# Adaptive vectors from one row sum of products per 128 outputs, and the short convolution's input projection with seven products of quarters

## The chip, the cores and the metric

The kernel runs on one core of a Trainium2 chip. Time is device time of one launch in microseconds (us). A row of a profile names engines: PE multiplies matrices, DVE (VectorE) and ACT (ScalarE) work element by element, POOL is GpSimd, SP issues most of the DMA transfers. A tile of the text "128x512" has 128 partitions of 512 elements; an instruction handles all partitions at once.

## What is computed

The reference is a backbone of two layers over 512 latent tokens of width 1024, with 256 context tokens ahead of layer 0. Cut to what the change touches:

```python
mod = silu(c) @ ada_w[layer] + ada_b[layer]        # 1024 -> 6144, per layer
shift_m, scale_m, gate_m, shift_f, scale_f, gate_f = split(mod, 6)
h = modulate(rms_norm(x), shift_m, scale_m)        # h * (1 + scale) + shift
# layer 0: attention and a gated recurrence on h @ ev_w_in, then @ ev_w_out
# layer 1: the short convolution
gate_b, gate_c, u = split(h @ od_w_in, 3)          # 1024 -> 3 * 1024
y = (gate_b * dwconv3(gate_c * u)) @ od_w_out
x = x + gate_m * y
h = modulate(rms_norm(x), shift_f, scale_f)
x = x + gate_f * ((gelu(dwconv3(a)) * val) @ ffn_w_down)   # a, val = split(h @ ffn_w_up, 2)
```

So each layer needs a vector `mod` of 6144 numbers, 48 columns of 128, and only the norms, the projections back and the final residual read it. All arithmetic is in fp32 to the outside. Inside, a product of matrices is made of three products: each operand is split into a high part and a low part (the rounding rest), and high times high, high times low and low times high are added up.

## The kernel before, in words

**Stages.** The profile shows them one after another: a prologue with the first 16 columns of layer 0's `mod`, the input norms and the projection of the first six heads' gates (0 to 65 us); the gated recurrence, woven by `Weave` with the remaining input projections (to about 245); attention, woven likewise (to about 380); the projection back `o0` (`project_back`, to 418); layer 0's up projection `ffn_up` (418 to 652); the projection back `d0` (652 to 784); the short convolution (784 to 917); its projection back `o1` (to 962); layer 1's up projection (to 1197); layer 1's down projection with the final norm.

**What sets the order.** Each engine runs its own queue in order. The queues come from the program's order through the tile framework, which also puts in the waits. A tile of a pool with `bufs=n` waits for the reader of the n-th tile before it. Weights come by one plan: `Weights._load` (L57) brings 1 MB at a time into two buffers `wraw`, `conv` (L69) casts a part to its high half `whi` on ACT (L92) and takes the rest `wlo` on DVE (L93), three buffers each, so conversions run a little ahead of the products. All three products are issued by `mm3` (L288 to L290).

**Adaptive vectors (`Ada`, L474 to L527).** All but the prologue's 16 columns are made in 160 units, eight for each of 20 jobs of 512 outputs. A unit loads 256 KB of `ada_w` (128 inputs by 512 outputs, three buffers `ar`), and DVE multiplies it by the 128 inputs (one number per partition) and adds it to `aa` (L502 for the first of eight, L504 for the others). After the eighth, DVE sums blocks of 32 partitions (`ad`, L508); three unit calls later PE sums the four blocks (`pad`, L514, with the constant `sel`), and two calls later DVE adds the bias from PSUM in four small additions (L520). The calls are scattered over the program: `ada_units` in the two weaves, `units(4)` or `units(5)` in each step of a projection back, `units(3)` after each pair of the short convolution, `units(2)` per group in layer 1's up projection.

**Up projection of an FFN.** The first four tiles go through `quad` (L1103). The rest goes in ten groups, `group` (L1151): a product of a 2x2 block matrix by seven products of quarters (Strassen's scheme, in Winograd's form with sums and differences of quarters), plus a plain product for the other half of the inputs. A group makes two pairs of output tiles and takes 84 half-width (256) and 48 full-width (512) matmuls. Its differences of weights are made on DVE by `_block` (L100; L108 to L114 the sums, L125 and L126 the casts), its differences of activations once per layer by `differences` (L1121). Results leave PSUM by copies (L1176) and additions (L1181, L1201).

**The short convolution.** `quad` makes the first two tiles of `gate_c` and of `u`; then ten calls of `pair` (L1095), each two tiles with 48 full-width matmuls: `gate_b` of j = 0, then `gate_c`, `u` and `gate_b` for j = 1 to 3. ACT copies `gate_c` to `cs` (L1287), DVE multiplies it by `u` (L1295), convolves (`conv3`, L1212 to L1214) into `sc`, and multiplies by `gate_b` (L1305), after which the result is split for `o1`.

**End of the prologue.** The products `pq` of the gates' projection (PE, `mm3`), then DVE makes `qh` from `pq` (L461), `gg` (L280), and, from `context` (L319), the modulated context tokens (L313, L314, L324). PE goes on with `pvl` (L577), the first product of the recurrence's stage. At the other end of the program L1323 and L1324 turn a gate vector into a row: a diagonal matrix `dgb` on DVE, multiplied by `ones` on PE into `pgb`, then copied to `gb` (L1325).

## Time and profile before

| | us |
|---|---|
| three runs before | 1333.11, 1334.85, 1336.33 (median 1334.85) |
| the profiled execution | 1333.99 |
| its span on the engines | 1332.2 |
| PE busy | 1304.5 |
| DVE busy | 965.4 |
| ACT busy | 625.2 |

The profiled execution lies 0.86 us below the median of the runs, and 1.8 us of it lie outside the span. In a row of a timeline stand start, duration, engine, line, operation, output<-inputs, the matmul's array, the output's shape and count, and in brackets the idle time before it and what ended that. A matmul's duration is longer than its pitch, the time to the next one's start, as PE overlaps them. A row of groups has the total, then the mean in ns of one, then idle time and what released it. A row of waits has the total, the number of times and the longest. A row of windows has for each engine its busy time and number of instructions, then the mean clock granted to PE (1.00 is full), the DMA engines' busy share and GB/s.

### The profile page before, as it was taken

To read this page: it belongs to the slowest core of one execution; us is meant where nothing else is said; L and a number is where in the kernel's file an instruction comes from. 1 tells how busy PE (TensorE), PEld (TensorE's weight loads), DVE (VectorE), ACT (ScalarE), POOL (GpSimd) and SP (SyncE) were. 2 spreads that over 40 slices of the span, in tenths; PEclk is the share of its full clock that TensorE was granted. 3 is DMA by queue.
4 is the path that set the end of the run, shared out by engine and by line. 5 is a ranking of instruction groups with operands and counts; after the bars stand their busy time and mean duration, and the time that the engine had idled before them with its cause. 6 is when DMAs were issued, how large, how long until landed. Compare 5 with 4: busy or idle time off the path is not lost. (4 is left out here: it accounts for less than half of the span.)

```text
span 1332.2 us, 21229 instructions
## 1 busy us (share of the span) xinstructions
PE 1304.5 (98%) x8456; PEld 1147.6 (86%) x8456; DVE 965.4 (72%) x1688; ACT 625.2 (47%) x1085; POOL 84.3 (6%) x87
## 2 busy tenths in 40 slices
PE   7999999999999999999999999999999999999997
PEld 4798888888779998889877898888999989899997
DVE  4668897887778878788766776667789897782333
ACT  4443445555545656565422253223456565663223
POOL 2204332311000000000000000000000000000000
PEclk9999999999999999999999999999999999999999
DMA  9842113674562122323466734555403423242231
GB/s 293 265 123 84 33 33 82 152 182 134 153 206 96 64 99 92 127 71 119 141 211 198 226 132 143 167 165 174 158 27 117 142 80 127 80 146 69 91 108 64
DMA packets 134995, 172.35 MB, mean 129 GB/s; under 512 B 14320, under 2 KB 103792, under 8 KB 129776
## 3 DMA queue, kind: packets, MB, share of 16 engines
q1 hardware_dynamic: 132896, 166.15, 39.3%
q10 hardware_dynamic: 2000, 4.85, 1.4%
q8 instruction: 66, 1.08, 0.3%
q14 instruction: 33, 0.27, 0.1%
HBM read 165.21 MB, written 2.10 MB: 126 GB/s over the span
## 5 line engine op out<-in xcount | busy, mean ns | idle before, releaser
L92 ACT CAST whi<-wraw 128x1024 fp32r<-128x1024 f32 (+1 forms) x122 | 124.1, 1021 | 280.8 <-PE pd L1340 70.4
L93 DVE TENSOR_TENSOR wlo<-wraw,whi 128x1024 fp32r<-128x1024 f32 (+1 forms) x122 | 145.2, 1192 | 107.7 <-ACT whi L92 107.1
L288 PE MATMUL p<-hf,whi 128*128 128x512 f32 (+1 forms) x640 | 215.4, 338 | 1.4 <-ACT whi L125 1.4
L290 PE MATMUL p<-hf,wlo 128*128 128x512 f32 (+1 forms) x640 | 214.6, 335 | 0.0
L289 PE MATMUL p<-hf,whi 128*128 128x512 f32 (+1 forms) x640 | 214.1, 335 | 0.0
L125 ACT CAST whi<-wraw 128x512 fp32r<-128x512 f32 (+1 forms) x160 | 113.0, 727 | 85.0 <-PE p L289 35.0
L290 PEld LDWEIGHTS p<-hf,wlo 128*128 128x128 f32 x640 | 120.1, 188 | 13.6
L288 PEld LDWEIGHTS p<-hf,whi 128*128 128x128 f32 x640 | 120.1, 188 | 12.3 <-ACT whi L125 1.6
L289 PEld LDWEIGHTS p<-hf,whi 128*128 128x128 f32 x640 | 120.1, 188 | 10.7
L126 DVE TENSOR_TENSOR wlo<-wraw,whi 128x512 fp32r<-128x512 f32 (+1 forms) x160 | 128.1, 817 | 0.9 <-ACT whi L125 0.5
L504 DVE SCALAR_TENSOR_TENSOR aa<-ar,sil,aa 128x512 f32<-128x512 f32 x140 | 104.8, 749 | 24.1 <-DMA ar<-in_ada_w_dram 21.8
L1339 PE MATMUL pd<-whi,g 128*128 128x256 f32 x352 | 98.2, 279 | 0.0
L1341 PE MATMUL pd<-wlo,g 128*128 128x256 f32 x352 | 98.1, 279 | 0.0
L1340 PE MATMUL pd<-whi,g 128*128 128x256 f32 x352 | 97.9, 278 | 0.0
L288 PE MATMUL pbd<-g,whi 128*128 128x512 f32 (+1 forms) x192 | 73.5, 383 | 0.0
L289 PE MATMUL pbd<-g,whi 128*128 128x512 f32 (+1 forms) x192 | 73.3, 382 | 0.0
L290 PE MATMUL pbd<-g,wlo 128*128 128x512 f32 (+1 forms) x192 | 73.1, 381 | 0.0
L288 PE MATMUL p<-T,whi 128*128 128x256 f32 x240 | 69.0, 288 | 0.0
L290 PE MATMUL p<-T,wlo 128*128 128x256 f32 x240 | 67.2, 280 | 0.0
L289 PE MATMUL p<-T,whi 128*128 128x256 f32 x240 | 67.2, 280 | 0.0
L1340 PEld LDWEIGHTS pd<-whi,g 128*128 128x128 f32 x352 | 66.3, 188 | 0.0
L1339 PEld LDWEIGHTS pd<-whi,g 128*128 128x128 f32 x352 | 66.1, 188 | 0.0
(679 smaller groups left out, 3296.3 us busy)
## 6 DMA issues: line engine op xcount, KB each, us to landing
ar<-in_ada_w_dram SPq DMA_DIRECT2D x160, 256.0 KB, 3.1
wraw<-in_upq_dram SPq DMA_DIRECT2D x40, 1024.0 KB, 4.8
wraw<-in_ffn_w_down_dram SPq DMA_DIRECT2D x16, 1024.0 KB, 5.3
wraw<-in_od_w_in_dram SPq DMA_DIRECT2D x12, 1024.0 KB, 5.6
wraw<-in_ev_w_in_dram SPq DMA_DIRECT2D x20, 512.0 KB, 5.2
araw<-in_ada_w_dram SPq DMA_DIRECT2D x16, 512.0 KB, 6.3
wraw<-in_ffn_w_down_dram SPq DMA_DIRECT2D x8, 768.0 KB, 4.7
wraw<-in_ev_w_out_dram SPq DMA_DIRECT2D x4, 1024.0 KB, 6.9
```

The source lines that it names most:

```text
L92: self.nc.scalar.copy(hv, rv)
L93: self.pin(self.nc.vector.tensor_tensor(lv, rv, hv.bitcast(F32), ALU.subtract))
L125: self.nc.scalar.copy(hi, src)
L126: V.tensor_tensor(lo, src, hi.bitcast(F32), ALU.subtract)
L288: TE.matmul(o, wh, mh, start=start, stop=False, skip_group_check=True)
L289: TE.matmul(o, wh, ml, start=False, stop=False, skip_group_check=True)
L290: TE.matmul(o, wl, mh, start=False, stop=stop, skip_group_check=True)
L504: pin(V.scalar_tensor_tensor(self.acc[:], raw[:], sil[:, r, 0:1], self.acc[:], ALU.mult, ALU.add))
L1339: TE.matmul(o[i][:, 0:256], gh[:, ts], w[0][:, k - k0], start=k == 0, stop=False)
L1340: TE.matmul(o[i][:, 0:256], gl[:, ts], w[0][:, k - k0], start=False, stop=False)
L1341: TE.matmul(o[i][:, 0:256], gh[:, ts], w[1][:, k - k0], start=False, stop=k == FT - 1)
```

## The change

**Adaptive vectors.** The weights are laid out transposed, so that a partition holds one output with its 1024 inputs: `adaT`, 512 KB for 128 outputs. A unit is one DVE instruction, `tensor_tensor_reduce` over 128x1024: it multiplies the weights by `silr`, a tile that holds silu(c) in every partition as a row, sums along the row onto the bias, and writes one column of `mod`. There are 80 units (32 columns of layer 0, 48 of layer 1), two buffers instead of three, and no `aa`, `ad`, `pad` or additions from PSUM. `silr` is made at the end of the prologue: eight diagonal matrices `dgs` on DVE (two buffers), eight products with `ones` on PE into `psr`, two copies on ACT. The calls become 6 in the first weave, 21 in the second, 2 per step of a projection back, 2 after the quad and 2 per half group of the short convolution, 1 per group in layer 1's up projection.

**Short convolution.** After the quad come five groups of `group` instead of ten pairs: `gate_c` and `u` for j = 1; `gate_b` for j = 0 and 1; `gate_c` and `u` for j = 2, then for 3; `gate_b` for j = 2 and 3. The weights are laid out for it (`odq`), the differences of activations are made in the quad (`differences("m", ...)`), and `short` holds the product and the convolution. A few constants move to another pool.

The diff, cut to its core:

```diff
+    plan += cols(od_in, D) + cols(od_in, 2 * D)
+    plan += [e for j in range(5) for e in quarters(a["odq"][j])]
...
+    silr = ap_.tile([P, D], F32, name="silr")
...
+        for j in range(2):
+            pt = aux_t(f"psr{j}")
+            for r in range(4):
+                dg = sp.tile([P, P], F32, tag="dgs", name=f"dgs{j}{r}", bufs=2)
+                V.tensor_scalar(dg[:], ident, sil[:, 4 * j + r, 0:1], None, ALU.mult)
+                TE.matmul(pt[:, r * P : (r + 1) * P], ones[:], dg[:], start=True, stop=True, skip_group_check=True)
+            S.copy(silr[:, j * T : (j + 1) * T], pt[:])
         for m in range(2):
             gate(m, pq[4 + m][:])
...
+            raw = ap_.tile([P, D], F32, tag="araw", name=f"ar{len(self.raw)}", bufs=2)
+            nc.sync.dma_start(raw[:], a["adaT"][l, c])
...
+            while len(self.raw) < min(self.n + 2, len(self.jobs)):
+                self.load()
...
+            pin(V.tensor_tensor_reduce(raw[:], raw[:], silr[:], 1.0, abT[:, l * 48 + c : l * 48 + c + 1], ALU.mult,
+                                       ALU.add, mod[:, l, c : c + 1]))
...
-    wv.add(ada_units(11, 6))
+    wv.add(ada_units(6, 11))
...
-    wv.add(ada_units(43, 3))
+    wv.add(ada_units(21, 6))
...
-                units(4 if len(groups) == 1 else 5)
+                units(2)
...
-                units(2)
+                units(1)
...
+    def short(m, c, u):
+        V.tensor_tensor(c[:], u[:], c[:], ALU.mult)
+        ts_[m] = gp.tile([P, T], F32, tag=f"g{16 + m}", name=f"sc{m}")
+        conv3(ts_[m], c, rowv(76 + m, 1), rowv(84 + m, 1), rowv(92 + m, 1), rowv(68 + m, 1))
...
+    oc, ou = quad("c", nrm.h, before, lambda: mv[1]())
+    for i in range(2):
+        t = fp.tile([P, T], F32, tag="t", name=f"cs{i}", bufs=5)
+        S.copy(t[:], oc[i][:])
+        short(i, t, ou[i])
+    units(2)
+    for n, js in enumerate(((1,), (0, 1), (2,), (3,), (2, 3))):
+        for i, (r0, r1) in enumerate(group(f"m{n}", mv[0])):
+            if len(js) == 1:
+                short(2 * js[0] + i, r0, r1)
+            else:
+                for j, r in zip(js, (r0, r1)):
+                    m = 2 * j + i
+                    V.tensor_tensor(r[:], r[:], ts_[m][:], ALU.mult)
+                    mix[m] = [gp.tile([P, T], F32R, tag=f"g{2 * m + z}", name=f"mc{m}{z}")[:] for z in range(2)]
+                    split(*mix[m], r[:])
+            units(2)
```

**The order of the instructions, at three places.** A row has the line, the operation, output<-inputs with a running number behind each name, and the shape. First PE at the end of the prologue, before: the last product of `pq`, then the first of the recurrence's stage.

```order
L288 MATMUL pq5_206<-h0_7_92,w0h7_493 128x512
L289 MATMUL pq5_206<-h0_7_92,w0h7_493 128x512
L290 MATMUL pq5_206<-h0_7_92,w0l7_494 128x512
L577 MATMUL pvl00_673<-whi0_581,h0_0_85 128x256
L578 MATMUL pvl00_673<-whi0_581,h0_0_85 128x256
L579 MATMUL pvl00_673<-wlo0_582,h0_0_85 128x256
```

The same place after the change (each line lies a little elsewhere, so that L288 is L289 and L577 is L558):

```order
L290 MATMUL pq5_208<-h0_7_94,w0h7_495 128x512
L291 MATMUL pq5_208<-h0_7_94,w0l7_496 128x512
L469 MATMUL psr0_629<-dgs00_630,ones_71 128x128
L469 MATMUL psr0_629<-dgs01_633,ones_71 128x128
L469 MATMUL psr0_629<-dgs02_636,ones_71 128x128
L469 MATMUL psr0_629<-dgs03_639,ones_71 128x128
L469 MATMUL psr1_643<-dgs10_644,ones_71 128x128
L469 MATMUL psr1_643<-dgs11_647,ones_71 128x128
L469 MATMUL psr1_643<-dgs12_650,ones_71 128x128
L469 MATMUL psr1_643<-dgs13_653,ones_71 128x128
L558 MATMUL pvl00_703<-whi0_583,h0_0_87 128x256
L559 MATMUL pvl00_703<-whi0_583,h0_0_87 128x256
```

Eight products `psr` now stand between `pq5` and `pvl00`; each reads one of the diagonal matrices `dgs`.

Next DVE at the same place, before: the modulated context (`ct`, `hc`), the heads' `qh` and the gates `gg`.

```order
L313 TENSOR_SCALAR ct0_199<-ct0_199,amul_81,mod_77 128x256
L461 TENSOR_TENSOR qh1_98<-pq1_202,sgq1_618 128x512
L314 TENSOR_TENSOR hc2_95<-ct0_199,hc0_93 128x256
L461 TENSOR_TENSOR qh2_99<-pq2_203,sgq2_621 128x512
L461 TENSOR_TENSOR qh3_100<-pq3_204,sgq3_624 128x512
L280 SCALAR_TENSOR_TENSOR gg0_627<-pq4_205,vec_76,gg0_627 128x512
L280 SCALAR_TENSOR_TENSOR gg1_630<-pq5_206,vec_76,gg1_630 128x512
L313 TENSOR_SCALAR ct0_199<-ct0_199,amul_81,mod_77 128x256
```

And after the change (L462 is L461 of before, L281 is L280; `dgs02` stands four rows above the first of these, ahead of `qh0`, and `dgs00` and `dgs01` near the start of the program):

```order
L314 TENSOR_SCALAR ct0_201<-ct0_201,amul_79,mod_76 128x256
L462 TENSOR_TENSOR qh1_100<-pq1_204,sgq1_620 128x512
L315 TENSOR_TENSOR hc2_97<-ct0_201,hc0_95 128x256
L462 TENSOR_TENSOR qh2_101<-pq2_205,sgq2_623 128x512
L462 TENSOR_TENSOR qh3_102<-pq3_206,sgq3_626 128x512
L468 TENSOR_SCALAR dgs03_639<-cst_70,sil_83 128x128
L468 TENSOR_SCALAR dgs10_644<-cst_70,sil_83 128x128
L281 SCALAR_TENSOR_TENSOR gg0_657<-pq4_207,vec_75,gg0_657 128x512
L468 TENSOR_SCALAR dgs11_647<-cst_70,sil_83 128x128
L281 SCALAR_TENSOR_TENSOR gg1_660<-pq5_208,vec_75,gg1_660 128x512
L468 TENSOR_SCALAR dgs12_650<-cst_70,sil_83 128x128
L468 TENSOR_SCALAR dgs13_653<-cst_70,sil_83 128x128
```

The last five of the eight matrices stand behind the four `qh`, three of them behind `gg0`, two behind `gg1`.

Last, DVE in the short convolution, just after the quad, before: `cs` is the product of `gate_c` and `u`, `sc` the convolution, `wlo158` the rest of the weights of a later pair.

```order
L1295 TENSOR_TENSOR cs00_8174<-ppc2_7934,cs00_8174 128x512
L1295 TENSOR_TENSOR cs01_8176<-ppc3_7935,cs01_8176 128x512
L93 TENSOR_TENSOR wlo157_8171<-wraw53_7773,whi157_8170 128x1024
L1213 SCALAR_TENSOR_TENSOR sc0_8179<-cs00_8174,vec_76,sc0_8179 128x511
L1213 SCALAR_TENSOR_TENSOR sc1_8184<-cs01_8176,vec_76,sc1_8184 128x511
L1214 SCALAR_TENSOR_TENSOR sc0_8179<-cs00_8174,vec_76,sc0_8179 128x511
L1214 SCALAR_TENSOR_TENSOR sc1_8184<-cs01_8176,vec_76,sc1_8184 128x511
L93 TENSOR_TENSOR wlo158_8191<-wraw54_8164,whi158_8190 128x1024
L504 SCALAR_TENSOR_TENSOR aa113_7723<-ar113_7716,sil_78,aa113_7723 128x512
L1305 TENSOR_TENSOR ppb00_8194<-ppb00_8194,sc0_8179 128x512
```

After the change (L1261 is L1295 of before, L1194 and L1195 are L1213 and L1214; L503 is the new unit, which the list shows in two rows; `wlo159` belongs to W1, the fourth block of weights of the first group):

```order
L1261 TENSOR_TENSOR cs0_7927<-ppc2_7653,cs0_7927 128x512
L1261 TENSOR_TENSOR cs1_7934<-ppc3_7654,cs1_7934 128x512
L126 TENSOR_TENSOR wlo158_7956<-wraw53_7492,whi158_7955 128x512
L1194 SCALAR_TENSOR_TENSOR sc0_7930<-cs0_7927,vec_75,sc0_7930 128x511
L1194 SCALAR_TENSOR_TENSOR sc1_7937<-cs1_7934,vec_75,sc1_7937 128x511
L1195 SCALAR_TENSOR_TENSOR sc0_7930<-cs0_7927,vec_75,sc0_7930 128x511
L1195 SCALAR_TENSOR_TENSOR sc1_7937<-cs1_7934,vec_75,sc1_7937 128x511
L503 ISA ar51_7441,mod_76<-ar51_7441,silr_86,vec_75 128x1024
L503 ISA mod_76 128x1
L503 ISA ar52_7941,mod_76<-ar52_7941,silr_86,vec_75 128x1024
L503 ISA mod_76 128x1
L126 TENSOR_TENSOR wlo159_7960<-wraw54_7916,whi159_7959 128x1024
```

Two units now stand ahead of the weights' rest `wlo159`, which the first group's fourth product needs.

More of the change, by code (lines that the diff above doesn't have):

```diff
@@ L255, in backbone @@
     mod = cp.tile([P, 3, 48], F32, name="mod")
-    sil = cp.tile([P, 8, 32], F32, name="sil")
     oml = cp.tile([P, 8], F32, name="oml")
@@ L474, in backbone @@
     class Ada:
[L477 to L478 removed]
+        jobs = [(0, c) for c in range(16, 48)] + [(1, c) for c in range(48)]
+        n, raw = 0, []
         def load(self):
[L481 to L486 removed]
@@ L507, in unit @@
-            red = ap_.tile([P, 16], F32, tag="ared", name=f"ad{self.n}", bufs=1)
-            V.tensor_reduce(red[:], self.acc[:].rearrange("p (b j) -> p b j", j=32), axis=AX.X, op=ALU.add,
-                            apply_transpose=True)
-            pm = []
-            def gather():
-                pm.append(aux(f"pad{l}{p_}{j}"))
-                TE.matmul(pm[0][:, 0:16], sel, red[:], start=True, stop=True)
-            def finish():
-                c = p_ * 8 + 4 * j
-                for qd in range(4):
-                    s4 = slice(32 * qd, 32 * qd + 32)
-                    V.tensor_tensor(mod[s4, l, c : c + 4], pm[0][s4, qd:16:4], abT[s4, l * 48 + c : l * 48 + c + 4],
-                                    ALU.add)
-                if p_ in (1, 4):
-                    w0 = (16 if p_ == 1 else 32) + 8 * l + 4 * j
-                    V.scalar_tensor_tensor(amul[:, 2 * l + (1 if p_ == 1 else 2), 4 * j : 4 * j + 4], mod[:, l, c : c + 4],
-                                           1.0, pv[:, w0 : w0 + 4], ALU.add, ALU.mult)
```

108 lines of the change are left out of this document (35 added, 73 removed).

## Prediction

> **What bounds the kernel now.** I read the page's first two lines, then PE's waits, then timelines and windows where a wait is long.
>
> ```profile
> span 1332.2 us, 21229 instructions
> PE 1304.5 (98%) x8456; PEld 1147.6 (86%) x8456; DVE 965.4 (72%) x1688; ACT 625.2 (47%) x1085; POOL 84.3 (6%) x87
> ```
>
> PE is busy for 1304.5 of 1332.2 us, so an edit pays by PE work that it takes away or by a wait of PE that it ends. PE's waits name the last work waited for:
>
> ```profile
> PE prx L412 <- ACT sqx L410: 5.1, 1, 5.1
> PE pad L514 <- DVE ad L508: 3.7, 2, 1.9
> PE p L288 <- ACT whi L125: 1.4, 2, 0.7
> ```
>
> The largest lies in the prologue and stays. The second is the adaptive vectors' own: twice PE waits for DVE to finish a job. DVE's share of 72% says little, since the stages differ. Windows over six of the FFN's groups and over the ten pairs of the short convolution show that (the tile rows give the ends of the first: copies of groups 2 and 8, six groups apart):
>
> ```profile
> 464.60:590.80 126.20, 126.20 (x793) 113.75 (x792) 100.38 (x163) 74.52 (x139) 0.00 (x0) 1.00 0.28 101
> 806.10:916.90 110.80, 110.80 (x491) 91.11 (x490) 75.84 (x109) 34.64 (x43) 0.00 (x0) 1.00 0.54 169
> L1176 ACT COPY R02t<-p x4: 352/368/380, 464.6 to 484.1; 128x256 f32<-128x256 f32 x4
> L1176 ACT COPY R08t<-p x4: 355/374/376, 590.8 to 610.6; 128x256 f32<-128x256 f32 x4
> ```
>
> PE has no idle time in either; the clock is 1.00. DVE is at 100.38/126.20 = 80% in the groups without any adaptive unit, and at 68% in the pairs with their units.
>
> **1. The row `silr` at the end of the prologue: +9.4.**
>
> ```profile
> 65.10 0.40 PE L290 MATMUL pq<-h,w0l 128*128 128x512 f32 x1
> 65.33 0.28 PE L577 MATMUL pvl<-whi,h 128*128 128x256 f32 x1
> 65.24 0.69 DVE L461 TENSOR_TENSOR qh<-pq,sgq 128x512 f32<-128x512 f32 x1
> 69.61 1.40 DVE L280 SCALAR_TENSOR_TENSOR gg<-pq,vec,gg 128x512 f32<-128x512 f32 x2
> 70.93 0.40 DVE L313 TENSOR_SCALAR ct<-ct,amul,mod 128x256 f32<-128x256 f32 x1
> L1323 DVE TENSOR_SCALAR dgb<-cst,mod x8: 276/282/287, 1037.9 to 1202.3; 128x128 f32<-128x128 f32 x8
> ```
>
> Now PE goes from `pq` to `pvl` without a gap. After the change eight `psr` stand between, each waiting for its `dgs`, and DVE has five of these behind the `qh`, two of them behind the last `gg`. `dgs02` needs the buffer that PE frees at about 65.4, and comes at about 65.8. From `qh0` to the first `gg` DVE takes 69.61 - 65.24 = 4.37, both `gg` 70.93 - 69.61 = 1.32. With six `dgs` at 0.2 each (the 282 ns rows, less some overlap) DVE ends at 65.8 + 4.37 + 1.32 + 1.2 = 72.7; a last product of about 0.3 and two hand-overs put `pvl` at 73.3, 8.0 later than 65.33. PE stands nearly all that time, and its clock may fall as in part 2 (1.4 us for one stretch): 9.4. Bounds: 6.5 (`dgs` that overlap wholly, no clock lost), 11 (two such stretches). ACT's two copies lie beside it.
>
> **2. The jobs' tails: -7.6 in `d0`, -4.0 elsewhere.** PE around the first long wait, DVE there, PE around the second, then two windows behind the waits:
>
> ```profile
> 666.16 0.39 PE L290 MATMUL pbd<-g,wlo 128*128 128x512 f32 x1
> 668.45 0.40 PE L514 MATMUL pad<-ad,cst 128*128 128x16 f32 x2 [1.91 <-DVE ad L508]
> 669.80 0.63 PE L288 MATMUL pbd<-g,whi 128*128 128x512 f32 x1
> 670.23 0.63 PE L289 MATMUL pbd<-g,whi 128*128 128x512 f32 x1
> 672.36 0.46 PE L288 MATMUL pbd<-g,whi 128*128 128x512 f32 x1
> 666.11 1.54 DVE L504 SCALAR_TENSOR_TENSOR aa<-ar,sil,aa 128x512 f32<-128x512 f32 x2 [2.94 <-DMA ar<-in_ada_w_dram]
> 699.86 0.40 PE L289 MATMUL pbd<-g,whi 128*128 128x512 f32 x1
> 702.07 0.36 PE L514 MATMUL pad<-ad,cst 128*128 128x16 f32 x2 [1.82 <-DVE ad L508]
> 706.35 0.52 PE L289 MATMUL pbd<-g,whi 128*128 128x512 f32 x1
> 668.00:672.00 4.00, 3.55 (x11) 2.82 (x12) 3.86 (x9) 0.00 (x0) 0.00 (x0) 0.64 0.58 194
> ```
>
> A row's load comes late, DVE waits 2.94 for it, and PE waits 1.91 for the sum. Then the clock is 0.64, and a matmul's pitch 670.23 - 669.80 = 0.43 instead of 0.23. From 666.16 to 672.36 PE starts 10 products in 6.20 us, where 10 x 0.23 = 2.3 would do: 3.9 lost. From 699.86 to 706.35, 12 in 6.49 instead of 2.8: 3.7. Together 7.6. The new unit gives PE nothing to wait for; a late load now holds DVE alone, with the weights' rest `wlo` behind it. That has half a step, 24 products of 0.23 or 5.5 us, in hand, so I take nothing for it.
>
> The other 18 `pad` cost as this one:
>
> ```profile
> 850.30 0.40 PE L290 MATMUL ppb<-hm,wlo 128*128 128x512 f32 x1
> 850.53 0.29 PE L514 MATMUL pad<-ad,cst 128*128 128x16 f32 x2
> 850.67 0.48 PE L288 MATMUL ppc<-hm,whi 128*128 128x512 f32 x1
> 850.98 0.39 PE L289 MATMUL ppc<-hm,whi 128*128 128x512 f32 x1
> ```
>
> 0.14 for itself, and 0.31 instead of 0.23 for its follower: 0.22, 18 times 4.0.
>
> **3. Groups for pairs: -4.7.** A group takes 126.20/6 = 21.03, five 105.2. The pairs take 110.8, of which four `pad` (0.9, counted above): 109.9. The difference is 4.7; the sevenths save little, since half of each product stays plain.
>
> **4. What a unit costs DVE.** No row has this instruction at 128x1024. The nearest also sums along a row, at 128x256, and the others give the step per element:
>
> ```profile
> L874 DVE CUSTOM_DVE_ANT_0 ps<-ps,bm,sm 128x256 f32<-128x256 f32 x32 | 15.3, 488 | 0.7
> L126 DVE TENSOR_TENSOR wlo<-wraw,whi 128x512 fp32r<-128x512 f32 x120 | 79.7, 684 | 0.9 <-ACT whi L125 0.5
> L126 DVE TENSOR_TENSOR wlo<-wraw,whi 128x1024 fp32r<-128x1024 f32 x40 | 48.6, 1216 | 0.0
> L504 DVE SCALAR_TENSOR_TENSOR aa<-ar,sil,aa 128x512 f32<-128x512 f32 x140 | 104.8, 749 | 24.1 <-DMA ar<-in_ada_w_dram 21.8
> 293.38 0.48 DVE L874 CUSTOM_DVE_ANT_0 ps<-ps,bm,sm 128x256 f32<-128x256 f32 x1
> 293.79 0.49 DVE L874 CUSTOM_DVE_ANT_0 ps<-ps,bm,sm 128x256 f32<-128x256 f32 x1
> ```
>
> 512 further elements take 1216 - 684 = 532 ns, 1.04 ns each; L874's pitch is 293.79 - 293.38 = 0.41. So 0.41 + 768 x 1.04 ns = 1.2 us. Bounds: 1.1 (a plain 1024 less its overlap), 1.95 (four of L874's 488). I take 1.2, by its own kind. [...]
>
> **5. The short convolution's start: +3.4.**
>
> ```profile
> 806.27 1.29 DVE L1295 TENSOR_TENSOR cs<-ppc,cs 128x512 f32<-128x512 f32 x2 [7.90 <-PE ppc L290]
> 808.71 1.41 DVE L1213 SCALAR_TENSOR_TENSOR sc<-cs,vec,sc 128x511 f32<-128x511 f32 x2
> 810.03 1.40 DVE L1214 SCALAR_TENSOR_TENSOR sc<-cs,vec,sc 128x511 f32<-128x511 f32 x2
> 441.10 0.28 PE L288 MATMUL p<-hf,whi 128*128 128x256 f32 x1
> 441.21 0.28 PE L289 MATMUL p<-hf,whi 128*128 128x256 f32 x1
> ```
>
> The quad ends at T0, 806.1 before. DVE's instructions overlap by some 0.08: two `sc` that show 1.41 start 810.03 - 808.71 = 1.32 before the next, 0.66 each, and a product of 512 takes 0.6 of its 684 ns. DVE then takes two `cs` (to T0 + 1.5), `wlo158` (0.6), four `sc` (4 x 0.66), two units (2.4) and `wlo159` (1.2): T0 + 8.3. PE has 36 half-width products at 441.21 - 441.10 = 0.115 (4.1) and the high parts that it can take first (2 x 0.23, 4 x 0.115, 2 x 0.23 = 1.4): T0 + 5.6. It waits 2.7. At half a chance of the 1.4 of lost clock, as in part 2, that is 3.4. Without the two units ahead of `wlo159` the wait would be 0.3; bounds 0 and 5. [...]
>
> **6. DVE in the groups: +2.5.** A group of the FFN takes 100.38/6 = 16.7 of DVE. Of that 4 x 0.66 + 4 x 0.6 = 5.0 are the gated tiles, and 11.7 remain. A group of `gate_c` and `u` adds two products and four `sc` (3.8), one of `gate_b` eight of 0.6 (4.8); each has four units, 4.8. That makes 20.3 and 21.3 against PE's 21.03, 103.5 of 105.2 for all five. DVE works in order, and the units stand right ahead of the next group's weights; followed row by row, PE waits some 1.5 to 3 us in all from the third group on. I take 2.5; bounds 0 and the rival below.
>
> **7. The rest: -0.7.** In the second weave 43 old units (43 x 0.66 = 28 and five sums) become 21 (25 us), a little less for DVE where PE seldom waits for it: between 0 and -3. `d0`'s and `o1`'s new units lie under PE's products.
>
> **Sum.** 9.4 - 7.6 - 4.0 - 4.7 + 3.4 + 2.5 - 0.7 = -1.7. The profiled execution of 1333.99 would become 1332.3; it lies 0.86 below the median of 1334.85, which becomes 1333.1.
>
> **Rivals.** First, slower: DVE sets the pace of the short convolution. Without units its five groups take DVE 103.5 - 24 = 79.5, so this begins where 20 units exceed 105.2 - 79.5, at 1.29 us each, close above my 1.2. [...] At 1.5 us it is 109.5: +4.3 instead of +2.5, and 0.6 in part 5: 1335.5. For it speaks that the sum is untried at 1024 and that DVE is full; against it L874's 0.41. Chance 0.22, of which 0.1 for the full double.
>
> Second, faster: PE's new waits are shorter than summed, as DVE has work in hand. Part 1 without lost clock is 8.0, part 5 2.0, part 6 nothing: 1.4 + 1.4 + 2.5 = 5.3 less, 1327.8. For it: the lost clock is carried over from two waits of another stage, and the gated tiles' work in part 6 can fall into PE's long plain products. Against it: the order in part 1 is fixed, so most of that wait stands. Chance 0.25.
>
> Third: `d0`'s waits don't go. The new unit has two buffers of 512 KB instead of three of 256 KB; if a load comes over 5.5 us late, DVE holds `wlo` long enough to stop PE. Then the 7.6 stay lost: 1340.7. Chance 0.08. That the groups save nothing (part 3 is zero, 1337.8) is part of the first.
>
> **Chances.** The forecast has 0.45, its own range 1330.5 to 1336.5. A measurement here tells about 0.2%, 2.7 us: faster is below 1332.2, slower above 1337.5. Faster: all of the second rival and 0.13 of the forecast, 0.38. Slower: 0.17 of the first rival, the third, 0.04 of the forecast: 0.29. The same: 0.33. The range goes from 1325 (the second rival with part 7 at -3) to 1342 (the third, and the first up to about 1.8 us); a full double of the unit is left out.
>
> **What would show it.** Right: a gap of 8 us ahead of `pvl` with `psr` in it; no `pad`; clock 1.00 all through `d0`; a wait of 2 to 3 us for W1's `wlo` behind the quad; five groups in 105 to 109 us; a unit of 1.2 us. Wrong: `pvl` close behind `pq`; units over 1.3 us with PE waiting for `wlo` in each group; long DMA waits of DVE in `d0` that PE shares.

## The result, and the profile after

The changed kernel takes 1345.85 us (median of four runs, 1343.44 to 1348.38) against 1334.86: the ratio is 1.0075, with a 95% interval of 1.0061 to 1.0089. It is 11 us slower, where 1.7 us faster was forecast, and it lies above the range. The profiled execution took 1343.44, the quickest of the four, with a span of 1341.7. The medians here are those of the undisturbed runs; the last experiment's kernel also had one slow run (1591.56 us at a clock of 0.75), which its median leaves out.

The page's first lines after the change:

```profile
span 1341.7 us, 21369 instructions
PE 1306.5 (97%) x8612; PEld 1158.7 (86%) x8612; DVE 969.4 (72%) x1685; ACT 647.8 (48%) x1151; POOL 85.7 (6%) x87
```

PE is no less busy than before (1304.5), and it waits more. Its longest waits now are, beside the one at `prx` that was there before:

```profile
PE psr L469 <- DVE dgs L468: 4.2, 2, 4.1
PE p00m L291 <- DVE wlo L126: 4.0, 3, 1.8
PE p00m L289 <- ACT whi L125: 1.6, 2, 1.2
```

The `pad` rows are gone. The first new row is the end of the prologue, the other two are the first of the weights' parts in the short convolution. To see where the time went I cut both profiled executions at the first PE instruction of each stage:

```
stage                               before  changed  difference
start to pvl                         65.33    73.16     +7.83
pvl to pf (recurrence, first part)   32.67    35.32     +2.65
pf to o0 (recurrence, attention)    264.96   264.68     -0.28
o0 with its norm                     55.39    56.58     +1.19
quad and groups, layer 0            234.11   234.24     +0.13
d0 with its norm                    131.17   121.56     -9.61
quad of the short convolution        22.71    22.98     +0.27
its pairs or groups                 110.80   114.45     +3.65
o1 with its norm                     45.05    45.85     +0.80
quad and groups, layer 1            235.06   234.72     -0.34
layer 1's down projection, end      134.93   138.11     +3.18
                                   1332.18  1341.65     +9.47
```

Two entries stand out: the last stage, whose code the change doesn't touch and of which no part of the prediction spoke, and the stretch from `pvl` to `pf`, for which part 1 held 1.4 us of lost clock and nothing else. Both windows of the last stage, before and after (the columns are the stretch and its length, then PE, weight loads, DVE, ACT, POOL, then clock, DMA share and GB/s):

```profile
1197.25:1332.18 134.93, 127.87 (x1103) 126.75 (x1101) 46.50 (x85) 41.60 (x80) 0.00 (x0) 0.98 0.26 86
```

```profile
1203.54:1341.65 138.11, 130.79 (x1099) 129.63 (x1097) 45.93 (x83) 40.91 (x80) 0.00 (x0) 0.99 0.25 84
```

The clock is all but the same (0.98 and 0.99), no new wait appears, and yet PE is busy for 3 us longer (127.87 and 130.79) with the same products. The timelines show it in the pitch. Two rows that follow each other, before and after:

```profile
1246.03 0.28 PE L1341 MATMUL pd<-wlo,g 128*128 128x256 f32 x1
1246.14 0.28 PE L1339 MATMUL pd<-whi,g 128*128 128x256 f32 x1
```

```profile
1252.82 0.28 PE L1318 MATMUL pd<-whi,g 128*128 128x256 f32 x1
1252.94 0.28 PE L1319 MATMUL pd<-wlo,g 128*128 128x256 f32 x1
```

A half-width product starts 0.113 us after the one ahead of it in the first and 0.120 in the second (the trace has it to the ns; the rows are rounded). Before, the products of gated tiles 0 to 5 stood at 0.120 and those of tiles 6 to 21 at 0.113; after, it is the other way round. The compiled programs show what changed: where the tiles lie in SBUF. The moved constants and the new buffers shift everything behind them by a few tens of bytes.

The two windows of the short convolution's groups and of `d0`, after the change:

```profile
663.98:781.57 117.59, 117.59 (x548) 97.75 (x547) 69.59 (x93) 33.02 (x38) 0.00 (x0) 1.00 0.64 211
808.52:922.97 114.45, 108.45 (x663) 96.16 (x661) 102.72 (x165) 53.28 (x99) 0.00 (x0) 0.99 0.52 176
```

In `d0` PE has no idle time left, and the clock is 1.00 throughout, as forecast. In the groups PE idles for 6.0 of 114.45 us, and DVE is busy for 102.72.

### The profile page after: what moved, and what is told of

Same layout as the page of the kernel before. It is cut to its first block, busy times and chain, and to the rows that moved or that the text cites. A ratio compares the mean times of both kernels' runs of the same rounds, so it can differ in the third digit from the quotient of the medians.

```text
span 1341.7 us, 21369 instructions
## 1 busy us (share of the span) xinstructions
PE 1306.5 (97%) x8612; PEld 1158.7 (86%) x8612; DVE 969.4 (72%) x1685; ACT 647.8 (48%) x1151; POOL 85.7 (6%) x87
## 4 chain that ended last, share of the span: by engine, by line
PE 77%; DVE 13%; DMA 4%; ACT 4%; issue 2%; SPq 0%; ACTq 0%; DVEq 0%
PE p L289 11%; PE p L290 10%; PE p L291 10%; PE pbd L289 3%; PE pbd L291 3%; PE pbd L290 3%; PE pd L1318 3%; PE pd L1319 3%; PE pd L1317 3%; DVE wlo L93 2%; DVE ar L503 1%; PE pq L289 1%; PE pq L290 1%; PE pq L291 1%; PE ppa L290 1%
## 5 line engine op out<-in xcount | busy, mean ns | idle before, releaser
L93 DVE TENSOR_TENSOR wlo<-wraw,whi 128x1024 fp32r<-128x1024 f32 (+1 forms) x102 | 120.2, 1183 | 133.9 <-ACT whi L92 133.5
L289 PE MATMUL p<-hf,whi 128*128 128x512 f32 (+1 forms) x640 | 215.5, 338 | 0.8 <-ACT whi L125 0.8
L92 ACT CAST whi<-wraw 128x1024 fp32r<-128x1024 f32 (+1 forms) x102 | 102.8, 1015 | 203.0 <-PE pd L1318 73.7
L125 ACT CAST whi<-wraw 128x512 fp32r<-128x512 f32 x200 | 141.3, 727 | 107.3 <-PE p L290 34.9
L126 DVE TENSOR_TENSOR wlo<-wraw,whi 128x512 fp32r<-128x512 f32 x200 | 160.0, 818 | 2.3 <-ACT whi L125 1.4
L289 PEld LDWEIGHTS p<-hf,whi 128*128 128x128 f32 x640 | 121.1, 189 | 12.0 <-ACT whi L125 1.2
L503 DVE CUSTOM_DVE_ANT_0 ar<-ar,silr,vec 128x1024 f32<-128x1024 f32 x80 | 100.5, 1279 | 5.2 <-DMA ar<-in_adaT_dram 5.0
L289 PE MATMUL pbd<-g,whi 128*128 128x512 f32 (+1 forms) x192 | 71.7, 373 | 0.0
L290 PE MATMUL pbd<-g,whi 128*128 128x512 f32 (+1 forms) x192 | 71.5, 372 | 0.0
L289 PE MATMUL p<-T,whi 128*128 128x256 f32 x240 | 68.9, 287 | 0.0
L1319 PEld LDWEIGHTS pd<-wlo,g 128*128 128x128 f32 x352 | 67.2, 191 | 0.0
```

The costliest lines, as they stand in the source:

```text
L92: self.nc.scalar.copy(hv, rv)
L93: self.pin(self.nc.vector.tensor_tensor(lv, rv, hv.bitcast(F32), ALU.subtract))
L125: self.nc.scalar.copy(hi, src)
L126: V.tensor_tensor(lo, src, hi.bitcast(F32), ALU.subtract)
L289: TE.matmul(o, wh, mh, start=start, stop=False, skip_group_check=True)
L290: TE.matmul(o, wh, ml, start=False, stop=False, skip_group_check=True)
```

## The experiments

Three theories for the loss, beside the start of the recurrence's stage, which nothing contradicts. D (distance): the pitch of half-width products depends on where the two operands start, and it is short when the starts differ by 64 modulo 128 bytes. U (units): the units of 1.2 us stand in DVE's queue ahead of the next weights, and PE waits for these. G (groups): the groups' own work fills DVE, whatever the units do. Rivals to D are M (multiples of 64 bytes are fast) and C (the pitch varies by execution). Each run's time stands beside that of the kernel before on the same chip.

### 32 bytes more

```diff
-    cst = cp.tile([P, 256], F32, name="cst")
+    cst = cp.tile([P, 264], F32, name="cst")
```

> The changed kernel with 32 more bytes per partition in the first pool, so that whi, wlo, the activations h and most gated tiles g start at 64 modulo 128 bytes (32 in the changed kernel; before, whi and wlo at 64, h and g at 0). The down projection of layer 1 was the same code and took 134.9 us before, 138.1 after; its 1056 half-width products stood at 113 ns before except for the first 6 of 22 gated tiles, and at 120 after except for those. Theory D (distance: the pitch is short when the two operands' starts differ by 64 modulo 128): whi and g are now equal, everything slow, down projection 140, time as after or 1 to 3 us above. Theory M (multiples of 64 are fast): down projection 134.9, and 4 to 7 us off the time. Theory C (the pitch varies by execution): no relation, 135 to 140 at random.

1351.47 us, ratio 1.0119 (1.0103 to 1.0135). The last stage:

```profile
1208.46:1348.02 139.56, 132.18 (x1099) 131.07 (x1097) 46.05 (x83) 40.92 (x80) 0.00 (x0) 0.98 0.25 83
```

139.6, as D said (140), and 4.7 over M's 134.9. Multiples of 64 bytes alone don't help. The whole kernel lost more than D gave it: 5.6 us over the changed kernel's 1345.85, instead of at most 3.

### 64 bytes more, further back

```diff
     silr = ap_.tile([P, D], F32, name="silr")
+    ap_.tile([P, 16], F32, name="gap")
```

> The changed kernel with 64 more bytes in the pool behind the weights' pool: whi and wlo stay at 32 modulo 128, h and all g go to 96. Theory D: the distance is 64 everywhere in the down projection of layer 1, so all of its products take 113 ns: 133.0 us against 138.1 after and 134.9 before; the first products of the recurrence's stage fall from 120 to 113 as well (1.2 us); 6 to 8 us off the time, to about 1339. Theory M: no multiple of 64 anywhere, 138 to 140, no gain. Theory C: 135 to 140 at random.

```profile
1209.18:1342.12 132.94, 125.66 (x1099) 124.56 (x1097) 46.00 (x83) 40.99 (x80) 0.00 (x0) 0.99 0.26 87
```

132.9: D again, 5.2 us off the changed kernel and below the kernel before. The whole kernel took 1346.11 (ratio 1.0081, 1.006 to 1.0102), no gain: in this execution `o1` took 50.0 us instead of 45.9, with a wait of 2.5 for DVE. The forecast of the whole was a miss, that of the stage was not.

### The kernel before, 64 bytes more

```diff
     yp = ctx.enter_context(tc.tile_pool(name="yp", bufs=1))
+    ap_.tile([P, 16], F32, name="gap")
```

> The kernel before with 64 more bytes in the pool behind the weights' pool: whi at 64, h and g at 64 instead of 0. Theory D: distance zero, all products of the down projection slow, 140 us against 134.9, the first products of the recurrence's stage at 120 instead of 113; the time 5 to 9 us above the kernel before, though no instruction differs. Theory M: everything at multiples of 64 as before, no change within 1 us. Theory C: no change beyond a scatter of 2 us.

1347.82 us, ratio 1.009 (1.0073 to 1.0107): 12 us for an unused tile of 64 bytes.

```profile
1207.69:1346.24 138.55, 131.74 (x1103) 130.66 (x1101) 46.37 (x85) 41.57 (x80) 0.00 (x0) 0.98 0.25 84
```

The last stage grows from 134.9 to 138.6, the groups of the two up projections by 2 us each, the short convolution's pairs by 1.7. M and C expected nothing. Against C also speaks that the stage repeats from kernel to kernel: 134.4 to 135.1 in the five that ran with the addresses of before, 138.1 to 138.3 in the three with those of the changed kernel.

### Eight buffers for dgs

```diff
-                dg = sp.tile([P, P], F32, tag="dgs", name=f"dgs{j}{r}", bufs=2)
+                dg = sp.tile([P, P], F32, tag="dgs", name=f"dgs{j}{r}", bufs=8)
```

> The changed kernel with eight buffers for dgs instead of two; DVE's list then has all eight matrices near the start of the program, PE's list is the same. If the gap ahead of pvl (7.8 us) and the slower products behind it come from DVE's order alone, pvl starts at 66.0 to 66.8 instead of 73.2 and the whole kernel is 7 to 9.4 us faster, about 1337. If the prologue pays for it (eight instructions of 0.2 on DVE ahead of the norms), 1.6 us of that are lost. If the work behind had absorbed the gap, as a faster start finds DVE late, less than 4 us are gained.

```profile
64.12 1.95 PE L469 MATMUL psr<-dgs,ones 128*128 128x128 f32 x16
66.75 0.39 PE L558 MATMUL pvl<-whi,h 128*128 128x256 f32 x1 [0.68 <-ACT silr L470]
```

The gap of 7.8 shrinks to 2.6: 1.95 for the products, 0.68 for ACT's copies, which I had put beside other work. `pvl` starts at 66.75, as expected, and `pf` starts at 101.2 instead of 108.5. The time is 1341.68 (1.0047, 1.0028 to 1.0067), 4 us less and not 7: in the profiled execution the short convolution took 117.1 and `o1` 51.1.

### Units moved

Ten of the 22 units of the short convolution stay, one per half group; ten go to layer 0's up projection.

```diff
-            if l and j < 9:
+            if j < 9 or not l:
                 units(1)
...
         short(i, t, ou[i])
-    units(2)
...
                     split(*mix[m], r[:])
-            units(2)
+            units(1)
...
-                units(2)
+                units(1 if nm == "o1" else 2)
```

> The changed kernel with its units placed elsewhere: one per half group of the short convolution instead of two, none right behind the quad, one per step of o1 instead of two, and one in each group of layer 0's up projection, which had none. Stage times after were 114.45 us for the short convolution's groups, 45.85 for o1, 211.2 for layer 0's groups; the groups without any wait would be 105.2. Theory U (the units, 1.2 us each in DVE's queue ahead of the next weights, make PE wait): short convolution 106 to 108, o1 45.2, layer 0's groups 211 to 212, the time 6 to 9 us below the changed kernel. Theory G (the groups' own work fills DVE and ACT, with or without units): short convolution stays over 111, time within 3 us of the changed kernel.

```profile
812.94:919.71 106.77, 106.14 (x662) 94.50 (x661) 90.60 (x144) 53.20 (x99) 0.00 (x0) 1.00 0.39 138
```

106.8 instead of 114.5, as theory U said and G did not. PE idles for 0.6 us. `o1` took 44.8. What I didn't expect: both layers' groups took 2.7 us more. Layer 1's had more units as well, seven instead of three, since the changed kernel runs out of its 80 units early in that stage. PE's new waits there are not for `whi` (0.6 and 0.4 us in all, 0.6 and 0.2 in the changed kernel) but for ACT's copies of results (`R`, L1157), 1.6 us in layer 0 and 2.0 in layer 1. 1342.25 us (1.0048, 1.0031 to 1.0066).

### Three mends

The last three edits of the changed kernel in one: 64 bytes further back, eight buffers, units moved.

> The moved units, eight buffers for dgs, and the 64 bytes behind the weights' pool, all in one. If the three causes are apart and add up: the start of the recurrence's stage 66.5 to 67 us instead of 73.2, the short convolution 106 to 108, the last stage 133, d0 118: against the kernel before 1.5 + 1 - 9.5 - 4 - 2 = 14 to 15 us faster, 1320 to 1322. If they hide one another (the units' place only mattered as DVE was late, the addresses give with one hand and take with the other), 1328 to 1334.

1330.84 us, ratio 0.996 (0.9948 to 0.9973): faster than the kernel before, but inside the second expectation, 1328 to 1334: the three mends don't add up. The short convolution took 106.3, the last stage 133.5 and `d0` 118, but layer 0's groups 214.7 and `o1` 49.3, where PE waited 1.8 and 0.9 us for the last group's results to be split (`mc`). In the profiled execution, the slowest of ten, `pvl` started at 68.4 instead of 66.5 to 67.

### The groups alone

The kernel before with the groups; the old vectors, three old units of 0.66 us per half group.

```diff
-            units(2)
+            units(3)
```

(The line is that of the changed kernel's inner loop, in the kernel before; the pairs, their plan and the units behind the quad go.)

> The kernel before with only the short convolution's groups; the adaptive vectors are the old ones, three old units of 0.66 us per half group and none behind the quad; no address moves. The old units are 30 x 0.66 = 20 us of DVE there, the new ones were 22 x 1.2 = 26. Theory U: W1's rest no longer stands behind units, PE waits some 0.3 there, and less than 2 us in all later: 107 to 109 us against 110.8 for the pairs, 2 to 4 us faster than the kernel before. Theory G: waits of 6 to 9 us as in the changed kernel, 112 to 115, slower than the kernel before by 1 to 4 us.

```profile
808.24:919.13 110.89, 107.23 (x671) 95.10 (x669) 99.61 (x167) 53.51 (x99) 0.00 (x0) 1.00 0.47 152
```

110.9, what the pairs took, between U's 107 to 109 and G's 112 to 115: PE idles for 3.7 us, which is what the products save (109.9 for the pairs without `pad`, some 106.2 for the groups). Three old units (2.0 us of DVE) hold up the weights about as much as two new ones do (2.4): behind the first group's start PE idles for 4.0 us in the changed kernel. In all 1340.03 us (1.0037, 1.0021 to 1.0052), as `o1` grew by 3.2 too.

### No units in the short convolution

As the three mends, but none there and none in `o1`, and three per step of `d0`.

```diff
                     split(*mix[m], r[:])
-            units(2)
...
-                units(2)
+                units({"o0": 2, "d0": 3, "o1": 0}[nm])
```

> As the one with three mends, but no unit at all in the short convolution and in o1; d0 has three per step instead of two. Theory U: the short convolution's groups run at PE's own pace, 105 to 106 us, o1 45; d0 takes 118 if three units a step have their loads in time, and 119 to 125 if DVE waits for them and the weights' rest with it. In all 1319 to 1322 in the first case, up to 1328 in the second. Theory G: short convolution over 110 still.

The short convolution took 106.5, no less than with one per half group, so those ten are hidden. That settles U against G: without any unit the groups' own work makes PE idle for 0.5 us. `d0` took 127.4 instead of 118: PE waited near its end,

```profile
785.70 0.58 PE L290 MATMUL pbd<-g,whi 128*128 128x256 f32 x1 [7.19 <-DVE xT L984]
```

and DVE had waited before it, once 2.2 us for `ar` and once 4.9 us for `whi`, whose weights came late (ACT waited 9.0 us for that load of `wraw`). 1343.15 us (1.0053, 1.0036 to 1.007): the prediction's third rival, forced by three units a step. The groups of the two up projections, with a unit behind nearly each, took 4.9 us more than in the changed kernel, and PE waited 3.1 and 3.5 us there for ACT's copies.

### The addresses back

Both paddings at once: `cst` with 264 columns and the tile `gap`, so that the weights' halves and the activations lie as before.

> The changed kernel with 32 bytes more in the first pool and 64 more in the pool behind the weights', so that whi and wlo start at 64, h and most gated tiles at 0 modulo 128 bytes as in the kernel before (the distance of 64); nothing else. If the addresses cost what theory D says: down projection of layer 1 134.9 instead of 138.1, the recurrence's first products (from pvl to pf) 33.5 to 34.3 instead of 35.3, quads 22.8 instead of 23.0; 4 to 6 us less than the changed kernel's 1345.9. The waits at the start of the recurrence's stage and in the short convolution stay. If less than 2 us come off, the rest of the loss lies in the waits alone.

The stages answer as expected: 134.4 instead of 138.1 at the end, 34.5 instead of 35.3 from `pvl` to `pf`, 22.8 instead of 23.0 in the quads, 5 us together. The time doesn't: 1345.54 (1.0081, 1.0055 to 1.0107), where 4 to 6 less than 1345.9 was expected. The groups took 119.3 and `o1` 49.7 in the profiled execution, with the same instructions in the same order.

```profile
808.93:928.21 119.28, 111.09 (x662) 98.43 (x661) 102.92 (x165) 53.21 (x99) 0.00 (x0) 0.96 0.50 169
```

PE idles for 8.2 us there, and the clock is 0.96; the longest wait, for `whi`, took 2.7 us.

### Units at idle places

```diff
         product(1, A, "S2", "T2")
         product(0, W, "W1", "X", gs=(1,))
         copy(1, A, 0, B)
+        units(fill)
         upto(9)
```

`fill` is 2 in the short convolution and 1 in the up projections, whose units behind the groups go, so that ten units instead of 22 remain in the short convolution, ten stand in layer 0's groups and seven in layer 1's; `silr` is made ahead of `ada_tile(0, 0)` with eight buffers; the addresses are back.

> Addresses as in the kernel before; silr made while PE waits for the first norm (its eight matrices and products ahead of the first column of mod, eight buffers); no units behind half groups: two in each group of the short convolution and one in each of the up projections, placed ahead of the addition for which DVE waits 4.2 us in every group; one per step of o1. If DVE's idle time there takes the units: short convolution 105 to 107, layer 0's groups 211, layer 1's 211 to 212, o1 45, pvl at 65.5 to 67.5, d0 118, last stage 135: 1319 to 1323, 13 to 16 us faster than before. If the prologue pays for silr in full: pvl at 68 to 69, 1322 to 1325. If the queue's order lets units hold the weights again: short convolution over 109.

1323.87 us, ratio 0.9923 (0.9897 to 0.9949): 11 us faster than before, and the lowest median of all. Its short convolution and last stage:

```profile
799.43:906.30 106.87, 106.26 (x663) 94.51 (x661) 93.06 (x148) 53.50 (x99) 0.00 (x0) 1.00 0.40 148
1185.91:1321.03 135.12, 127.63 (x1101) 126.36 (x1099) 46.30 (x84) 41.18 (x80) 0.00 (x0) 0.98 0.26 86
```

The other stages came within 1.2 us of their numbers: layer 0's groups 212.2, `d0` 118.5, `o1` 45.0; `pvl` started at 63.9, ahead of its range. For the short convolution this doesn't tell the place of the units from their number, as ten behind the half groups did as well (106.8). For the up projections it does, with nine or ten units in layer 0's groups and seven in layer 1's both times. Layer 0's groups took 213.9 us with the units behind them and 212.2 with the units ahead of the addition; layer 1's took 2.7 and 0.2 us more than in the changed kernel. (Putting the addresses back moves each by 0.2.)

### The vectors alone

The changed kernel with the ten pairs back, two new units behind each, and the addresses back.

> The changed kernel with the short convolution's ten pairs back, two new units behind each, and the addresses back; so the adaptive vectors alone. By the stages: the start of the recurrence's stage +9.4, d0 -9.5, the pairs without their pads 109.9 instead of 110.8, o1 and o0 between 0 and +1: 1334 to 1338, no change against the kernel before. If the new units make PE wait behind pairs too, as behind half groups: pairs 113 or more and 1339 to 1342.

1336.23 us, ratio 1.0002 (0.9991 to 1.0013): no change. The pairs:

```profile
808.26:918.13 109.87, 109.87 (x483) 90.15 (x481) 74.39 (x99) 34.56 (x43) 0.00 (x0) 1.00 0.61 195
```

109.87 where 109.9 was worked out: without their `pad`, and with PE never idle. Two units behind a pair harm nothing, since DVE has 32% of that stage free.

### All gated tiles at the same distance

As the one with idle places, with 96 more bytes in the pool of gated tiles 0 to 5.

> The one with units at idle places, and 96 more bytes in the pool of the first six gated tiles, which then start at 0 modulo 128 like the other sixteen (96 before and after). Theory D: with all 22 at a distance of 64 from the weights' halves, the last stage has no slow product left: 133.0 to 133.2 us against 135.1, its groups of four input tiles all at 113 ns. The same buffers hold the quads' first weights, which then stand at distance 0 from h; if that counts for weights as the held operand too, each of the three quads grows from 22.8 to 23.2, as it did where the distance was 0 or 32. In all 1321 to 1324, even with or 2 us below the one with units at idle places. If the last stage stays at 135, the distance isn't what the pitch goes by.

```profile
1189.04:1322.49 133.45, 125.95 (x1101) 124.56 (x1099) 46.24 (x84) 41.23 (x80) 0.00 (x0) 0.98 0.26 87
```

133.5, and in the trace all but a few of its half-width products stand at 113 or 114 ns. The quads grew by 0.1 each, less than the 0.4 that I feared. In all 1325.59 us (0.9927, 0.9904 to 0.995), not told apart from the one without it. In the profiled execution the recurrence's stage started at 67.9 instead of 63.9: PE waited 2.6 us for the first `h` instead of 1.2, and the clock was 0.76 from 20 to 30 us, where it had been 1.00.

## Why the prediction was wrong, point by point

**Part 1, the row `silr`: right.** PE and DVE at the place:

```profile
65.69 0.49 PE L469 MATMUL psr<-dgs,ones 128*128 128x128 f32 x2 [0.16 <-DVE dgs L468]
70.25 3.25 PE L469 MATMUL psr<-dgs,ones 128*128 128x128 f32 x10 [4.07 <-DVE dgs L468]
73.16 0.56 PE L558 MATMUL pvl<-whi,h 128*128 128x256 f32 x1
74.16 0.41 PE L559 MATMUL pvl<-whi,h 128*128 128x256 f32 x1
74.37 0.41 PE L560 MATMUL pvl<-wlo,h 128*128 128x256 f32 x1
```

```profile
65.35 0.28 DVE L468 TENSOR_SCALAR dgs<-cst,sil 128x128 f32<-128x128 f32 x1 [0.74 <-PE psr L469]
69.92 0.47 DVE L468 TENSOR_SCALAR dgs<-cst,sil 128x128 f32<-128x128 f32 x2
71.95 0.60 DVE L468 TENSOR_SCALAR dgs<-cst,sil 128x128 f32<-128x128 f32 x2
```

`pvl` starts at 73.16 for a forecast 73.3, and its first products stand at 0.21 (74.37 - 74.16) instead of 0.115: the clock was 0.65 up to 76 us. With the addresses of before, the stretch from `pvl` to `pvc` grew from 10.91 to 12.22, so 1.3 for the 1.4.

**Part 2: right.** `d0` with its `pad` gone is 9.6 shorter, where 7.6 and its share of the other 18 were forecast. The third rival came only where three units a step were forced on it.

**Part 3: nearly right by itself, but not received in this kernel.** In the four kernels whose groups hardly wait (units moved, three mends, no units, idle places), PE is busy for 105.9 to 106.3 us there, where 105.2 was forecast. The pairs take 109.9, so the products save 3.6 to 4.0 of the 4.7.

**Part 4: right.** All 80 units show

```profile
L503 DVE CUSTOM_DVE_ANT_0 ar<-ar,silr,vec 128x1024 f32<-128x1024 f32 x80 | 100.5, 1279 | 5.2 <-DMA ar<-in_adaT_dram 5.0
```

1279 ns, with a pitch of 1.20 (in the next rows), where a plain difference of that size (`wlo`, L126) takes 1216. So L874's 0.41 and 1.04 ns per element were the right measure. No run shows a unit at the full double to which the first rival gave 0.1 of its chance: the rows of three experiments (eight buffers, three mends, no units) have it at 1.28 us too.

**Part 5: right in its chain, a little high in its price.** DVE and PE behind the quad, which ends at 808.52:

```profile
813.00 1.28 DVE L503 CUSTOM_DVE_ANT_0 ar<-ar,silr,vec 128x1024 f32<-128x1024 f32 x1
814.20 1.28 DVE L503 CUSTOM_DVE_ANT_0 ar<-ar,silr,vec 128x1024 f32<-128x1024 f32 x1
815.41 1.82 DVE L126 TENSOR_TENSOR wlo<-wraw,whi 128x1024 fp32r<-128x1024 f32 x2
```

```profile
816.68 0.50 PE L291 MATMUL p00m<-hm,wlo 128*128 128x512 f32 x1 [1.60 <-DVE wlo L126]
```

`wlo` is there at T0 + 8.2 for a forecast 8.3, and PE loses 2.6 of a forecast 2.7. That the loss fits so well is in part luck: the wait for `wlo` is 1.60, another of 0.42 for ACT's copy `Rm0r` was not forecast, and 0.6 lie in PE's own products. The clock stays at 1.00 behind this wait (816.7 to 830 us), so the 0.7 for lost clock didn't come.

**Part 6: this term failed, and with it the first rival's threshold.** DVE's work was right (102.72 us for 103.5), and so was the order: the units stand right ahead of the next group's weights. What this order costs PE was mis-sized: 2.5 us, with a larger loss only from 1.29 us per unit, where DVE's work would exceed PE's. The loss came at 1.20, with DVE's work still below PE's. At the start of the third group, on DVE, ACT and PE:

```profile
851.68 1.28 DVE L503 CUSTOM_DVE_ANT_0 ar<-ar,silr,vec 128x1024 f32<-128x1024 f32 x1
852.89 0.69 DVE L110 TENSOR_TENSOR wraw<-wraw 128x512 f32<-128x512 f32 x1
```

```profile
853.61 2.09 ACT L125 CAST whi<-wraw 128x512 fp32r<-128x512 f32 x3
```

```profile
854.28 0.39 PE L289 MATMUL p00m<-hm,whi 128*128 128x256 f32 x1 [1.16 <-ACT whi L125]
```

The unit holds the sum of weights (L110), this holds the cast, and the cast holds PE. At the start of the fifth group a second cause, for which the sum had no term, joins the first. DVE (`ws` is a sum of quarters of the weights), then PE:

```profile
895.50 0.69 DVE L108 TENSOR_TENSOR ws<-wraw 128x512 f32<-128x512 f32 x1 [2.69 <-DMA wraw<-in_odq_dram]
898.03 1.28 DVE L503 CUSTOM_DVE_ANT_0 ar<-ar,silr,vec 128x1024 f32<-128x1024 f32 x1
899.24 1.28 DVE L503 CUSTOM_DVE_ANT_0 ar<-ar,silr,vec 128x1024 f32<-128x1024 f32 x1
900.44 1.89 DVE L126 TENSOR_TENSOR wlo<-wraw,whi 128x512 fp32r<-128x512 f32 x3
```

```profile
901.19 0.58 PE L291 MATMUL p00m<-hm,wlo 128*128 128x256 f32 x1 [1.81 <-DVE wlo L126]
```

The weights themselves came late here: DVE, though nearly full, stood idle for 2.69 us until they landed, then two units went ahead of `wlo`. Behind PE's wait of 1.81 the clock was 0.54 from 901 to 903 us, and the 15 products from 901.19 to 904.55 took 3.36 us instead of some 1.8.

Together the groups lost 114.45 - 105.2 - 2.6 = 6.6 us in this execution instead of 2.5. Of this 4.0 are PE's idle time in four waits, some 1.6 the lower clock behind the last of them, and 1.0 the products of part 3.

The five kernels with these units in this place took 160 to 169 us for the groups and `o1` together. With ten units in the groups the two took 151.5 to 151.8 (units moved, idle places, the last experiment), or 155.6 (three mends, where `o1` grew); without any, 151.5. So that the units cost PE this time is shown; that two of them per half group are too many is shown too, but not how much of it is their place.

Why the same instructions spread by 9 us from kernel to kernel stays open, but the traces show what goes with it. In the groups, DVE's waits for loads of the weights were 3.0, 3.5, 4.0, 4.6 and 5.6 us in the kernels whose groups took 114.3, 114.5, 116.3, 117.1 and 119.3, and at most 0.8 in the kernels with ten units or none. (There ACT waits for these loads instead, 6 to 12 us, and PE idles for 0.5 or 0.6.) The rows of these waits in the changed kernel and in the one with the addresses back:

```profile
DVE ws L108 <- DMA wraw<-in_odq_dram: 3.5, 2, 2.7
DVE ws L108 <- DMA wraw<-in_odq_dram: 5.6, 3, 3.1
```

In `o1` DVE's longest wait for `whi`, which waits for a load of `ffn_w_up`, was 3.7 or 3.8 us where the stage took 45.7 to 45.9, and 5.3 to 6.0 where it took 49.7 to 51.1. SP often issues such a load only when a `wlo` has freed its buffer (in the changed kernel it waited for that five times in the groups, 12.6 us in all, and five times in `o1`, 12.4 us), so units ahead of `wlo` may put it off. The units' own loads are also under way at that time: one was out from 886.2 to 891.4 us, the late load of the fifth group from 888.2 to 895.5. No run tells these two causes apart.

**Part 7 and the cover.** The second weave gave 0.3 of the 0.7. That `d0`'s and `o1`'s units lie under PE's products held: PE has no idle time in `d0`, and `o1` with the same units, but behind pairs, took 44.6 us (45.05 before). The 0.8 that `o1` grew by in the changed kernel are waits of 0.4 and 0.5 near its end, where DVE is late by a load of weights and no unit is near. `o0` grew by 1.2, for which the forecast had nothing; as it took 57.0 in the kernel with the old units and the groups, this isn't shown to come from the new ones.

**What no part held: the addresses.** With 3.2 at the end, 0.8 or more from `pvl` to `pf` and 0.6 in the quads, 4 to 5 us. The prediction has no term for the diff's small moves (constants to another pool, two buffers for three), and so put them at nothing without a reason.

Against the forecast the spans are 11.2 us off, 9.5 slower where 1.7 faster was forecast. Part 6 holds 4.1 of this, the addresses 4 to 5, and `o0` and `o1` 2.0; the rest are small terms of both signs.

The medians don't split in the same way. The vectors alone change nothing (1.0002). The groups on top of them, with the addresses of before, make the whole loss (1.0081), some 10 us where a gain of 4.7 less small waits was forecast; with the old vectors the groups lose 4 to 5 us (1.0037). Moved addresses alone cost the kernel before 12 us, but putting them back in the changed kernel gained 5 us in the stages and nothing in the median (1.0075 and 1.0081). So their cost is shown by stage, not as a share of this loss. The profiled execution of the changed kernel was the quickest of its four, that with the addresses back one of the slower of six; that the others wait longer in the groups is likely, but they left no trace.

## What to carry to other kernels

An engine that takes its queue in order is not to be priced by its share of busy time: ask of each added instruction what stands directly behind it and who waits for that, the next load of a buffer included (here DVE was busy for 102.7 of 114.5 us in the groups, and PE idled for 6.0). Put it where the engine would have idled, as here ahead of an addition for which DVE, in the changed kernel, waited 4.1 or 4.2 us in 15 of the 20 groups of the up projections (2.3 to 3.0 in the other five, at most 3.4 in those of the short convolution), and leave slack where the engine is nearly full. `silr`, built with two buffers, put `pvl` off by 7.8 us; eight buffers left 2.6 us ahead of it, and building it where PE idles anyway left none (`pvl` at 63.9, before the change at 65.33). When a pool's sizes change and start addresses move, compare the pitch of untouched products (here 113 and 120 ns) before looking for waits.

## What was not expected of the hardware

Half-width products, with the gated tiles or activations as held operand and the weights' halves as the moving one, have two pitches, 113 and 120 ns, by the operands' start addresses. In the last stage the short one went with starts that differ by 64 modulo 128 bytes, and the long one with 0 and 32, in each of the five layouts that ran: whi at 64 with g at 0 or 96 (before), at 32 with 32 or 96 (changed), at 64 with 64 or 96 (32 bytes more; the kernel before with 64 more), at 32 with 96 throughout (64 bytes more, further back), and at 64 with 0 throughout (the last experiment). The stage took 132.9 to 133.5 where all starts differed by 64, and 138.6 to 139.6 where none did. With the activations held (`pvl`) it was 113 before, with whi at 64 and h at 0, and 120 from 76 us on in the changed kernel, with both at 32. Where the weights are the held operand (groups, quads) the mean pitch lies at 115 to 120 ns in these two kernels with no such clear rule. Why the distance matters stays open.
